# Memory attention's query projection as seven block products per head, with its weight sums made in DRAM

## The chip, the cores and the metric

The kernel runs on one core of one Trainium2 chip. The metric is the device time of one execution in microseconds, the median of several runs. The core has five engines that run their own instruction streams and meet at semaphores: TensorE (PE in the profile; its weight loads are PEld), VectorE (DVE), ScalarE (ACT), GpSimd (POOL) and SyncE (SP), which here only issues transfers. GpSimd also issues transfers, those that add to their destination among them.

## What is computed

One layer of a decoder, 512 positions wide, with 1024 channels, in float32. In short:

```python
h = rms_norm(x, norm_mix)
q_a, k_a, v_a, u_b, gate_b, gate_c, g_a, g_b = split(h @ w_in)
o_a = stick_breaking_attention(heads(q_a), heads(k_a), heads(v_a))     # 8 heads of 64, causal
y_b = gate_b * causal_conv3(gate_c * u_b)
x = x + (sigmoid(g_a) * (o_a @ w_branch_a) + sigmoid(g_b) * (y_b @ w_branch_b)) @ w_mix_out
# memory sublayer: 4 heads of 256, 256 memory tokens
q = rms_norm(x, norm_mem_q) @ w_mem_q
k, v = split(rms_norm(mem, norm_mem_kv) @ w_mem_kv)
x = x + (softmax(q @ k.T / 16) @ v) @ w_mem_o
gate, up = split(rms_norm(x, norm_ffn) @ w_ffn_in)                      # hidden width 2816
x = x + (silu(gate) * up) @ w_ffn_out
out = rms_norm(x, norm_final)
```

## The kernel before, in words

**Precision.** Every float32 operand of a matmul is split into a high part (a cast to float32r, on ScalarE) and the rest (a subtraction, on VectorE). A product is then three matmuls, high by high, high by rest and rest by high (`mm3`, lines 159 to 161). `load_w` (line 142 on) does this for a weight tile of 128 by 1024: a load on the SyncE queue into `wr` (line 146), the cast `wh` (154) and the rest `wl` (155). Each of the three tags has four buffers. `split` does it for activations (177 and 179). Activations lie transposed, channels on partitions and the 512 positions along the free dimension, so one projection of 128 output channels is 8 channel blocks x 3 terms = 24 matmuls of 512 columns (`gemm`).

**Order of the stages.** First the values of the causal attention, then the attention itself, in 16 steps (the loop at line 594). In each step TensorE works on projections (`project`) between the scores and the weighted sums, GpSimd masks (`causal`, line 415), ScalarE and VectorE make the weights. Then comes the merge loop (line 637 on), eight rounds of two gates and one branch projection, whose result is `merged`. After it, in this order: memory keys (`km`, line 662 on, eight column blocks, a 512-wide and a 256-wide part, lines 668 and 671); memory values (`vm`, two halves of four weight tiles); the mixing projection with the residual (`residual` with `w_mix_out`, line 733 on), which also makes the normalized input `x1g` of the queries; then the four heads of memory attention, the output projection with its residual (`residual` again, this time with `forms_of`), and the feed-forward.

**Memory queries.** `mem_q(h)` makes the two 128-channel blocks of head h by two plain `gemm`s (48 matmuls of 512 columns). The first head's run ahead of the loop; those of head h + 1 are emitted in head h between the softmax and the transposes of the probabilities (line 833), so that TensorE has work while VectorE finds the maxima (807) and ScalarE the exponentials (817).

**Seven products.** The feed-forward already uses, for each 2 by 2 block product, seven block products in place of eight, in a form whose partial sums are shared (Winograd's variant of Strassen's scheme). The blocks are pairs of channel blocks and halves of the positions, so a product has a free dimension of 256 (`product`, lines 913 to 921). `forms_of` (line 703 on) makes the seven activation forms, and the order of use, the PSUM banks and the evictions are written out by hand. Products 0, 3, 4 and 5 accumulate in bank `z`, 1 in `v`, 2 and 6 in `y`. Evictions copy a running sum out of `z` (line 950) between products.

**Sums in DRAM.** The seven products need sums of weight blocks. For the second feed-forward weight they are made in DRAM ahead of their use: for each of 11 column groups `sums_step` issues, in four steps, two copies on the SyncE queue (768 KB and 256 KB, line 568) and three adding transfers on the GpSimd queue (512, 256 and 256 KB, line 572), each waiting for the one before. `tick()` starts one step for up to four groups. It is called in each of the eight rounds of the merge, twice in the memory keys and four times in the first residual.

**Order on the queues.** A scheduler orders each engine's instructions by the order of emission and by estimated times, except in hand-ordered stretches such as the feed-forward; `after(i, earlier)` fixes an order without a wait.

Of the kernel before, what the change touches and what calls it, by code (L numbers as in the profile page):

```python
# [8 lines left out]
F32 = mybir.dt.float32  # L9
# [4 lines left out]
P = 128  # L14
# [28 lines left out]
def hybrid_layer(ctx: ExitStack, tc: tile.TileContext, xT_d, memT_d, mem_d, cols_d, wv_d, win_d,  # L43
# [18 lines left out]
    def nm(s):  # L62
        count[0] += 1
        return f"{s}{count[0]}"
# [490 lines left out]
        nc.gpsimd.dma_start(d.rearrange("o (t p) -> p (o t)", p=P), rm)  # L555
        return rm, d

    sums = [dpool.tile([P, 4, 512], F32, tag=f"sums{j}", name=nm("sums")) for j in range(NJ)]
    ticks = [0]

    def slots(j, i, n=1):
        return wfo_d[j].rearrange("p (s c) -> p s c", s=4)[:, i:i + n, :]

    def sums_step(j, n, *last):
        t = sums[j]
        if n == 0:
            for to, of, k in ((1, 1, 3), (0, 3, 1)):
                after(nc.sync.dma_start(t[:, to:to + k, :], slots(j, of, k)), last)
            return
        to, of = ((t[:, 0:4:3, :], slots(j, 0, 2)), (t[:, 1:2, :], t[:, 0:1, :]),  # L570
                  (t[:, 2:3, :], t[:, 1:2, :]))[n - 1]
        after(nc.gpsimd.dma_start(to, of, accum_op=ALU.add), last)  # L572

    def tick(*last):
        for n in range(3, -1, -1):
            if 0 <= ticks[0] - n < NJ:
                sums_step(ticks[0] - n, n, *last)
        ticks[0] += 1

    fill = []  # L580
    for p in range(TT):
# [9 lines left out]
    g(*args)  # L591
    scores(*steps[0])
    settle_behind()
    for i in range(len(steps) + 1):
        if i in MEM_AT:
            mem_square(MEM_AT.index(i))
        if i == MEAN_AT:
            rm, rmd = mem_factors()
        if i == ROW_AT:
            rmb = cpool.tile([P, MEM], F32, tag="rmb", name="rmb")  # L600
            after(nc.gpsimd.dma_start(rmb, rmd.broadcast_to([P, MEM])), exps[-1:])
        some = []
# [12 lines left out]
        if i > 0:  # L615
            values(*steps[i - 1])
        settle_behind(*exps[-1:], *joined[-1:])
# [44 lines left out]
    km, ready = [], []  # L662
    for m in range(KD):
        w = load_w(wmk_d[m])
        after(lows[-1], ready[m - 4:m - 3] if m > 3 else ())
        ps = mmtile("km")
        for k in range(KD):
            nc.tensor.matmul(ps, w[0][:, k, :], mgs[k], start=k == 0, stop=False,
                             skip_group_check=True)
        for k in range(KD):  # L670
            nc.tensor.matmul(ps[:, :MEM], w[1][:, k, :], mg[k][0], start=False, stop=k == KD - 1,
                             skip_group_check=True)
        t = tmp("km", MEM)
        nc.scalar.copy(t, ps[:, MEM:])
        ready.append(nc.vector.tensor_tensor(out=t, in0=ps[:, :MEM], in1=t, op=ALU.add))
        nc.vector.tensor_tensor(out=t, in0=t, in1=rmb, op=ALU.mult)
        if m % 2 == 0:
            pair = unit("kmh"), unit("kml")
        hi, lo = (u[:, (m % 2) * MEM:(m % 2 + 1) * MEM] for u in pair)
        nc.scalar.copy(hi, t)  # L680
        nc.vector.tensor_tensor(out=lo, in0=t, in1=f(hi), op=ALU.subtract)
        km.append((hi, lo))
        if m % 4 == 3:
            tick(ready[-1])
        if m == 0:
            merged.append(split(sig[0], "m"))
    vm = [[None] * 2 for _ in range(MT)]
    for n in range(2):
        pss = [ztile("vm") for _ in range(MT)]
        for c in range(4):  # L690
            w = load_w(wmv_d[n, c], 512)
            if n == 0:
                after(lows[-1], ready[c + 4:c + 5])
            for j in range(2):
                k = 2 * c + j
                for t in range(MT):
                    sl = slice(t * P, (t + 1) * P)
                    mm3(pss[t], (mg[k][0][:, sl], mg[k][1][:, sl]),
                        (w[0][:, j, :], w[1][:, j, :]), k == 0, k == KD - 1)
        for t in range(MT):  # L700
            vm[t][n] = split(pss[t], "vm", rm[:, t:t + 1])

    def forms_of(xe, xo):

# [28 lines left out]
    def residual(w_dram, act, old, gain, pairs=False):  # L733


        xs, xn = [], []
        acc = tmp("acc")
        for m in range(KD):
            w = load_w(w_dram[m])
# [6 lines left out]
                xm = old[m]  # L746
            nc.vector.tensor_tensor(out=xm, in0=ps, in1=xm, op=ALU.add)
            xs.append(xm)
            if pairs:
                raw = f(unit("xr"))  # L750
                nc.scalar.activation(raw, xm, AF.Copy, scale=gain[:, m:m + 1])
                if m % 2:
                    xn.append(forms_of(even, raw))
                else:
                    even = raw
            else:
                xn.append(split(xm, "xg", gain[:, m:m + 1]))
                if m % 2:
                    tick(lows[-1])
# [6 lines left out]
        return xs, xn, (lambda: squares_mean(acc, TT))  # L766
# [8 lines left out]
    def mem_q(h, between=None):  # L775
        got = []
        for j in range(2):
            if j and between:
                midway.append(between)
            w = load_w(wmq_d[2 * h + j])  # L780
            ps = mmtile("mq")
            gemm(ps, w, x1g)
            got.append(split(ps, "mq"))
        return got

    r1s = []
    q_next = mem_q(0, lambda: r1s.append(mean1[1]("r1", log_exp_tables(sigmoid))))
    r1 = r1s[0]
    r1s = cpool.tile([P, TT], F32, tag="r1s", name="r1s")
    nc.vector.tensor_scalar(out=r1s, in0=r1, scalar1=(D // MH) ** -0.5, scalar2=None, op0=ALU.mult)  # L790
    for h in range(MH):
        q = q_next
        scs = []
        for t2 in range(2):
            ps = ztile("sc")
# [8 lines left out]
        for t2 in range(2):  # L804
# [5 lines left out]
            nc.vector.scalar_tensor_tensor(out=nb, in0=mx, scalar=-1.0,  # L810
                                           in1=r1s[:, 2 * t2:2 * t2 + 2], op0=ALU.mult,
                                           op1=ALU.mult)
            pr = tmp("pr")
# [8 lines left out]
            for i in range(2):  # L822
                nc.vector.tensor_scalar(out=pr[:, i * MEM:(i + 1) * MEM],
                                        in0=pr[:, i * MEM:(i + 1) * MEM],
                                        scalar1=rs[:, i:i + 1], scalar2=None, op0=ALU.mult)
            prs.append(pr)
        if h + 1 < MH:
            q_next = mem_q(h + 1)
        pt = [otile("pt") for _ in range(MT)]
        for t in range(TT):  # L830
            for m in range(MT):
                c = (t % 2) * MEM + m * P
                nc.tensor.transpose(pt[m][:, t * P:(t + 1) * P], prs[t // 2][:, c:c + P], ident)
        ptr = [split(pt[m], "pt") for m in range(MT)]
        for j in range(2):
            ps = ztile("om")
            c = h * 256 + j * P
# [6 lines left out]
    x2T, x2f, mean2 = residual(wmo_d, om, x1, g_ffn, True)  # L844

# [252 lines left out]
        rest_of(*one_cast(j))  # L1098

    def w01(j):  # L1100
        return j, slots(j, 1, 2), 0, 1

    def w23(j):
        return j, sums[j][:, 0:2, :], 2, 3
# [372 lines left out]
def _layout(x, mem, norm_mix, w_in, conv_w, w_branch_a, w_branch_b, w_mix_out, norm_mem_q,  # L1477
# [12 lines left out]
    def by_pair(w):  # L1490


        return w.reshape(KD // 2, 2, P, 2, NF, P).transpose(4, 2, 3, 1, 0, 5).reshape(NF, P, 2048)

    gains = np.stack([norm_mix[0], norm_mem_q[0], norm_mem_kv[0], norm_ffn[0]])
    columns = np.concatenate([gains.reshape(4 * KD, P), conv_w[0].reshape(3 * TT, P)])
    q = w_ffn_out[0].reshape(NJ, 2, P, 2, 512)
# [11 lines left out]
        "w_mem_q": by_column(w_mem_q[0]),  # L1509
# [26 lines left out]
```

## Time and profile before

| | |
|---|---|
| median of 3 runs | 839.47 us (839.43 to 840.65) |
| the profiled execution | 839.78 us, its span 838.1 us |
| granted TensorE clock | 0.998 |
| HBM read, written | 136.74 MB, 25.17 MB |
| transfers of sums: first and last issue | 187.7 us, 370.8 us |
| query matmuls, first and last | 388.8 us, 449.0 us |

The page gives the busy time of each engine and, in forty slices, how it is spread; a matmul's own duration (about 390 ns for 512 columns) is longer than its spacing, since matmuls overlap, so spacing is read from the chain or the timeline and not from the mean duration. Busy time by stage shows which engine fills a stage. The list of waits names who waited for whom. The chain that ended last goes back from the end through whatever released each step.

### The profile page before, as it was taken

To read this page: it belongs to the slowest core of one execution; us is meant where nothing else is said; L and a number is where in the kernel's file an instruction comes from. 1 tells how busy PE (TensorE), PEld (TensorE's weight loads), DVE (VectorE), ACT (ScalarE), POOL (GpSimd) and SP (SyncE) were. 2 spreads that over 40 slices of the span, in tenths; PEclk is the share of its full clock that TensorE was granted. 3 is DMA by queue.
4 is the path that set the end of the run, shared out by engine and by line. 5 is a ranking of instruction groups with operands and counts; after the bars stand their busy time and mean duration, and the time that the engine had idled before them with its cause. 6 is when DMAs were issued, how large, how long until landed. Compare 5 with 4: busy or idle time off the path is not lost.

```text
span 838.1 us, 11942 instructions
## 1 busy us (share of the span) xinstructions
PE 829.5 (99%) x4374; PEld 713.9 (85%) x4374; DVE 662.4 (79%) x1086; ACT 463.5 (55%) x796; POOL 107.7 (13%) x131
## 2 busy tenths in 40 slices
PE   9999999999999999999999999999999999999996
PEld 7888888888888888788888889999999999888885
DVE  7879899996544466555455698999999999999886
ACT  7567868674332354444444565645555555576664
POOL 0011131111111111110000022111111110000401
PEclk9999999999999999999999999999999999999999
DMA  8552444239999999982431326667777763575552
GB/s 302 154 166 101 123 113 104 71 108 311 247 220 245 218 244 292 289 229 87 145 104 51 99 52 156 165 187 193 195 185 191 189 178 101 161 218 198 178 187 101
DMA packets 56109, 143.69 MB, mean 171 GB/s; under 512 B 6289, under 2 KB 7569, under 8 KB 56050
## 3 DMA queue, kind: packets, MB, share of 16 engines
q1 hardware_dynamic: 43410, 119.43, 43.1%
q0 software_dynamic: 12352, 23.21, 18.2%
q8 instruction: 34, 0.56, 0.3%
q10 hardware_dynamic: 288, 0.28, 0.1%
q14 instruction: 25, 0.20, 0.1%
HBM read 136.74 MB, written 25.17 MB: 193 GB/s over the span
## 4 chain that ended last, share of the span: by engine, by line
PE 95%; DMA 3%; DVE 1%; ACT 1%; issue 0%; DVEq 0%; ACTq 0%; SPq 0%
PE z L918 13%; PE p L1229 12%; PE pr L159 8%; PE pr L160 8%; PE pr L161 8%; PE y L913 5%; PE r L160 3%; PE r L159 3%; PE r L161 3%; DMA wr<-in_w_mem_v_dram 3%; PE v L286 3%; PE y L921 2%; PE v L913 2%; PE mq L161 2%; PE mq L159 2%; PE mq L160 2%
## 5 line engine op out<-in xcount | busy, mean ns | idle before, releaser
L154 ACT CAST wh<-wr 128x1024 fp32r<-128x1024 f32 x84 | 87.8, 1050 | 149.2 <-issue 71.4
L155 DVE TENSOR_TENSOR wl<-wr,wh 128x1024 fp32r<-128x1024 f32 x84 | 102.9, 1227 | 38.5 <-ACT wh L154 38.4
L159 PE MATMUL pr<-xgh,wh 128*128 128x512 f32 x288 | 112.7, 391 | 0.0
L160 PE MATMUL pr<-xgl,wh 128*128 128x512 f32 x288 | 112.4, 390 | 0.0
L161 PE MATMUL pr<-xgh,wl 128*128 128x512 f32 x288 | 112.3, 390 | 0.0
L161 PEld LDWEIGHTS pr<-xgh,wl 128*128 128x128 f32 x288 | 54.0, 188 | 11.5
L159 PEld LDWEIGHTS pr<-xgh,wh 128*128 128x128 f32 x288 | 54.1, 188 | 10.7
L160 PEld LDWEIGHTS pr<-xgl,wh 128*128 128x128 f32 x288 | 54.1, 188 | 10.5
L866 POOL DMA_DIRECT2D ws<-in_w_ffn_in_dram x22 | 26.6, 1209 | 270.4 <-DMA ws<-in_w_ffn_in_dram 55.0
L918 PE MATMUL z<-xd,wf 128*128 128x256 f32 x360 | 47.5, 282 | 0.0
L950 ACT COPY sa<-z 128x256 f32<-128x256 f32 x44 | 16.4, 374 | 51.8 <-PE z L918 51.8
L918 PEld LDWEIGHTS z<-xd,wf 128*128 128x128 f32 x360 | 45.0, 190 | 0.1
L1010 DVE TENSOR_TENSOR wf<-wg,wf 128x1024 fp32r<-128x1024 f32 (+1 forms) x44 | 43.1, 979 | 1.5
L1010 DVE TENSOR_TENSOR wl<-wr,wh 128x1024 fp32r<-128x1024 f32 x33 | 41.0, 1243 | 3.3 <-ACT wh L1077 3.3
L1077 ACT CAST wh<-wr 128x1024 fp32r<-128x1024 f32 x33 | 34.5, 1049 | 7.2 <-DMA wr<-sums 3.3
L366 DVE TENSOR_TENSOR g<-pr,r0b 128x512 f32<-128x512 f32 x16 | 11.0, 689 | 34.1 <-PE pr L161 34.1
L918 PE MATMUL z<-xf,wf 128*128 128x256 f32 x264 | 35.4, 283 | 0.0
L918 PE MATMUL z<-xc,wf 128*128 128x256 f32 x264 | 35.1, 282 | 0.0
L918 PEld LDWEIGHTS z<-xf,wf 128*128 128x128 f32 x264 | 33.4, 192 | 0.1
L918 PEld LDWEIGHTS z<-xc,wf 128*128 128x128 f32 x264 | 33.0, 190 | 0.0
L572 POOL DMA_DIRECT2D sums<-sums x22 | 19.3, 878 | 102.1 <-DMA sums<-in_w_ffn_out_dram 74.0
L1010 DVE TENSOR_TENSOR wf<-ws,wf 128x1024 fp32r<-128x1024 f32 (+1 forms) x23 | 26.9, 1171 | 0.0
(353 smaller groups left out, 2208.5 us busy)
## 6 DMA issues: line engine op xcount, KB each, us to landing
wr<-in_w_in_dram SPq DMA_DIRECT2D x36, 512.0 KB, 4.1
ws<-in_w_ffn_in_dram SPq DMA_DIRECT2D x22, 512.0 KB, 4.9
wg<-in_w_ffn_in_dram SPq DMA_DIRECT2D x22, 512.0 KB, 4.3
ws<-in_w_ffn_in_dram POOLq DMA_DIRECT2D x22, 512.0 KB, 5.9
wr<-sums SPq DMA_DIRECT2D x22, 512.0 KB, 4.2
sums<-in_w_ffn_out_dram SPq DMA_DIRECT2D x11, 768.0 KB, 10.5
wr<-in_w_ffn_out_dram SPq DMA_DIRECT2D x16, 512.0 KB, 4.5
sums<-in_w_ffn_out_dram POOLq DMA_DIRECT2D x11, 512.0 KB, 10.0
```

The costliest lines, as they stand in the source:

```text
L154: after(nc.scalar.copy(h2, raw), lead[-1:])
L155: lows.append(nc.vector.tensor_tensor(out=l2, in0=raw, in1=f(h2), op=ALU.subtract))
L159: nc.tensor.matmul(ps, a[0], b[0], start=start, stop=False, **kw)
L160: nc.tensor.matmul(ps, a[0], b[1], start=False, stop=False, **kw)
L161: nc.tensor.matmul(ps, a[1], b[0], start=False, stop=stop, **kw)
L286: nc.tensor.matmul(vps[t], xg[k][a][:, sl], wv[k][b], start=k == 0 and (a, b) == (0, 0), stop=k == KD - 1 and a == 1)
L866: nc.gpsimd.dma_start(s13, a[:, 0:4:3, :], accum_op=ALU.add)
L913: nc.tensor.matmul(ps, hi, both[0], start=i < 3 and k == 0, stop=False, skip_group_check=True)
L918: nc.tensor.matmul(ps[:, :HS], a, b, start=i < 3 and k == 0 and j == 0, stop=k == KP - 1 and j == 2, skip_group_check=True)
L1010: nc.vector.tensor_tensor(out=lo, in0=src, in1=f(hi), op=ALU.subtract)
L1077: nc.scalar.copy(hi, raw)
L1229: nc.tensor.matmul(res[i][s2], a[:, ts], b, start=j == 0 and n == 0, stop=n == 2 and j == (BEHIND - 1 if (i, s2) == (5, 1) else NJ - 1))
```

## The change

The diff does five things.

1. **Queries as seven products.** For each head the 1024 by 256 weight is taken as 2 by 2 blocks (rows in pairs of channel blocks, columns in two halves of 128), and the product with the activations, also in 2 by 2 blocks (pairs of channel blocks, halves of the positions), is made as 7 products x 4 row pairs x 3 terms, all of 256 columns. `q_product` issues one product and its eviction. Its order in a head is 0, 1, 3, 2, 4 (`mem_q_first`) and, later, 5, 6 (`mem_q_last`). The first matmul of a product is ordered behind the product before it (`turn`), as are the transposes between `mem_q_first` and `mem_q_last` of the next head. The sign of every second key block is turned, to match a form that comes out negated.
2. **Forms of the activations.** `flat_forms` makes the seven forms in the first residual, as `forms_of` does in the second.
3. **Forms of the weights.** Each head's weight sums are made in DRAM by two copies and three adding transfers (`form_sums`), started in the attention loop: head h's copies at step 2 + 2h, and each adding step two steps of the loop later. `pair_forms` loads and splits three and a half tiles of 128 by 1024 a head, in place of two.
4. **When the output sums run.** `tick` is now called at every step of the attention loop, in every round of the merge, once per head and four times in the second residual; it is no longer called in the keys and in the first residual. Of the 11 groups of the second feed-forward weight, the first five start in the merge, one a round from the first on; the other six start at its last round, the four heads, and the second residual's first call.
5. **Order of the stages.** The mixing projection with its residual now comes right behind the merge, whose last `merged` tile is split in the merge itself. Then come the keys, the first half of the values, the first five products of head 0, half of the second half of the values, products 5 and 6, and the rest of the values. The keys take their banks from the pool of four and no longer from the pool of two.

The core of it, lines left out at "...":

```diff
+    def form_sums(t, src):
+        w = quarters(src)
+        return ([copied(t[:, 0:2, :], w[:, 0:2, :]), copied(t[:, 2:4, :], w[:, 1:3, :])],
+                [added(t[:, 0:2, :], w[:, 3:4, :].broadcast_to([P, 2, 512]))],
+                [added(t[:, 2:3, :], t[:, 0:1, :])], [added(t[:, 3:4, :], t[:, 2:3, :])])
...
+    qsums = [in_dram(f"qsums{h}") for h in range(MH)]
+    for h in range(MH):
+        job(2 + 2 * h, form_sums(qsums[h], wmq_d[h]), 2)
+    for j in range(5):
+        job(len(steps) + 1 + j, out_sums(j))
+    for j in range(5, NJ):
+        job(len(steps) + 3 + j, out_sums(j))
+
     for i in range(len(steps) + 1):
+        tick(*exps[-1:])
...
-        if m < KD - 1:
-            merged.append(split(sig[0], "m"))
+        merged.append(split(sig[0], "m"))
         tick(sigmoid)
...
-        if m % 4 == 3:
-            tick(ready[-1])
-        if m == 0:
-            merged.append(split(sig[0], "m"))
...
-    x1, x1g, mean1 = residual(wmix_d, merged, None, g_q)
+    x1, x1f, mean1 = residual(wmix_d, merged, None, g_q, flat_forms)
...
+    def q_product(h, i):
+
+        if i == 0:
+            qbanks[h] = {"z": ztile("qz"), "t": tmp("qa"), "u": tmp("qb"), "s": tmp("qs")}
+        elif i in (1, 2):
+            qbanks[h]["vy"[i - 1]] = mmtile("qv")
+        b = qbanks[h]
+        ps = b["zvyzzzy"[i]][:, :HS]
+        for k in range(KD // 2):
+            hi, lo = (w[:, k * P:(k + 1) * P] for w in forms_w[h, i])
+            xh, xl = x1f[k][i]
+            for j, (u, x) in enumerate(((hi, xh), (hi, xl), (lo, xh))):
+                mm = nc.tensor.matmul(ps, u, x, start=i < 3 and k + j == 0,
+                                      stop=k == KD // 2 - 1 and j == 2, skip_group_check=True)
+                if k + j == 0:
+                    after(mm, turn[-1:])
+        turn.append(mm)
...
+        if i == 0:
+            qacts.append(nc.scalar.copy(s[:, :HS], ps))
+        elif i == 1:
+            nc.vector.tensor_tensor(out=t[:, :HS], in0=ps, in1=s[:, :HS], op=ALU.add)
+        elif i == 3:
+            qacts.append(nc.scalar.copy(s[:, HS:], ps))
+        elif i == 4:
+            qacts.append(nc.scalar.copy(u[:, HS:], ps))
...
+        elif i == 6:
+            nc.vector.tensor_tensor(out=t[:, HS:], in0=ps, in1=s[:, HS:], op=ALU.add)
+            qgot[h][0] = split(t, "mq")
...
-        ps = mmtile("km")
+        ps = ztile("km")
...
+    values_part(0, (0, 1, 2, 3))
+    for n in range(3):
+        pair_forms(0, n)
+    mem_q_first(0)
+    values_part(1, (0, 1))
+    q_product(0, 5)
+    q_product(0, 6)
+    values_part(1, (2, 3))
+    for n in range(2):
+        pair_forms(1, n)
...
+        if 0 < h + 1 < MH:
+            pair_forms(h + 1, 2, bound)
+        tick(*casts[-1:])
         if h + 1 < MH:
-            q_next = mem_q(h + 1)
+            mem_q_first(h + 1)
...
+        if h + 1 < MH:
+            mem_q_last(h + 1)
```

More of the change, by code (lines that the diff above doesn't have):

```diff
@@ L556, in mem_factors, with quarters, in_dram, copied @@
         return rm, d
[L558 to L572, printed above, removed]
+    def quarters(w):
+        return w.rearrange("p (s c) -> p s c", s=4)
+    def in_dram(tag):
+        return dpool.tile([P, 4, 512], F32, tag=tag, name=nm(tag))
+    sums = [in_dram(f"sums{j}") for j in range(NJ)]
+    def copied(to, of):
+        return lambda *last: after(nc.sync.dma_start(to, of), last)
+    def added(to, of):
+        return lambda *last: after(nc.gpsimd.dma_start(to, of, accum_op=ALU.add), last)
+    def out_sums(j):
+        t, w = sums[j], quarters(wfo_d[j])
+        return ([copied(t[:, 1:4, :], w[:, 1:4, :]), copied(t[:, 0:1, :], w[:, 3:4, :])],
+                [added(t[:, 0:4:3, :], w[:, 0:2, :])], [added(t[:, 1:2, :], t[:, 0:1, :])],
+                [added(t[:, 2:3, :], t[:, 1:2, :])])
+    def form_sums(t, src):
[3 more added lines that the diff above has]
+                [added(t[:, 2:3, :], t[:, 0:1, :])], [added(t[:, 3:4, :], t[:, 2:3, :])])
+    jobs, started = {}, [0]
+    def job(at, steps, lag=1):
+        for n, some in enumerate(steps):
+            jobs.setdefault(at + n * lag, []).extend(some)
     def tick(*last):
[L575 to L578, printed above, removed]
+        for some in jobs.pop(started[0], ()):
+            some(*last)
+        started[0] += 1
     fill = []
@@ L748, in residual @@
             xs.append(xm)
[L749 to L755, printed above, removed]
-            else:
-                xn.append(split(xm, "xg", gain[:, m:m + 1]))
-                if m % 2:
-                    tick(lows[-1])
+            if old is not None and m % 2:
+                tick(lows[-1])
+            raw = f(unit("xr"))
+            nc.scalar.activation(raw, xm, AF.Copy, scale=gain[:, m:m + 1])
+            if m % 2:
+                xf.append(formed(even, raw))
+            else:
+                even = raw
             if m == 0:
@@ L765, in residual @@
                 nc.vector.tensor_tensor(out=acc, in0=acc, in1=sq, op=ALU.add)
[L766 to L768 removed]
+        return xs, xf, (lambda: squares_mean(acc, TT))
+    x1, x1f, mean1 = residual(wmix_d, merged, None, g_q, flat_forms)
     mean1 = mean1()
     fpool = ctx.enter_context(tc.tile_pool(name="fpool", bufs=2))
[L773 to L784 removed]
@@ L786, in hybrid_layer, with pair_forms @@
-    r1s = []
-    q_next = mem_q(0, lambda: r1s.append(mean1[1]("r1", log_exp_tables(sigmoid))))
+    forms_w = {}
+    def pair_forms(h, n, *last):
+        t, w = qsums[h], quarters(wmq_d[h])
+        src, which = ((w[:, 1:3, :], (0, 1)), (t[:, 2:4, :], (3, 6)), (t[:, 0:2, :], (2, 4)),
+                      (w[:, 0:1, :], (5,)))[n]
+        raw = wpool.tile([P, 2, 512], F32, tag="wr", name=nm("wr"))
+        if n == 3:
+            both = wpool.tile([P, 2, 512], F32R, tag=("wh", "wl")[h % 2], name=nm("wf"))
+            raw, hi, lo = raw[:, 0:1, :], both[:, 0:1, :], both[:, 1:2, :]
+        else:
+            hi, lo = (wpool.tile([P, 2, 512], F32R, tag=t, name=nm("wf")) for t in ("wh", "wl"))
+        nc.sync.dma_start(raw, src)
+        after(nc.scalar.copy(hi, raw), qacts[-1:])
+        after(nc.vector.tensor_tensor(out=lo, in0=raw, in1=f(hi), op=ALU.subtract), last)
+        for n, i in enumerate(which):
+            forms_w[h, i] = hi[:, n, :], lo[:, n, :]
@@ new lines, in mem_q_first, with mem_q_last @@
+    def mem_q_first(h):
+        q_product(h, 0)
+        pair_forms(h, 3)
+        q_product(h, 1)
+        q_product(h, 3)
+        q_product(h, 2)
+        q_product(h, 4)
+    def mem_q_last(h):
+        q_product(h, 5)
+        if h + 1 < MH:
+            pair_forms(h + 1, 0)
+        q_product(h, 6)
+        if h + 1 < MH:
+            pair_forms(h + 1, 1)
+    qacts, turn, km, ready = [], [], [], []
+    r1s = []
+    for m in range(KD):
+        w = load_w(wmk_d[m])
+        after(lows[-1], ready[m - 4:m - 3] if m > 3 else ())
+        ps = ztile("km")
+        for k in range(KD):
+            nc.tensor.matmul(ps, w[0][:, k, :], mgs[k], start=k == 0, stop=False,
+                             skip_group_check=True)
+        for k in range(KD):
+            nc.tensor.matmul(ps[:, :MEM], w[1][:, k, :], mg[k][0], start=False, stop=k == KD - 1,
+                             skip_group_check=True)
+        t = tmp("km", MEM)
+        nc.scalar.copy(t, ps[:, MEM:])
+        ready.append(nc.vector.tensor_tensor(out=t, in0=ps[:, :MEM], in1=t, op=ALU.add))
+        nc.vector.scalar_tensor_tensor(out=t, in0=t, scalar=1.0 - 2 * (m % 2), in1=rmb,
+                                       op0=ALU.mult, op1=ALU.mult)
+        if m % 2 == 0:
+            pair = unit("kmh"), unit("kml")
+        hi, lo = (u[:, (m % 2) * MEM:(m % 2 + 1) * MEM] for u in pair)
+        nc.scalar.copy(hi, t)
+        nc.vector.tensor_tensor(out=lo, in0=t, in1=f(hi), op=ALU.subtract)
+        km.append((hi, lo))
+        if m == 1:
+            r1s.append(mean1[1]("r1", log_exp_tables(sigmoid)))
```

109 lines of the change are left out of this document (66 added, 43 removed).

## The prediction

> **What bounds the kernel now.** I read the page's engine totals and slices first, then busy time by stage, then the waits of TensorE, then the chain that ended last.
>
> ```profile
> span 838.1 us, 11942 instructions
> PE 829.5 (99%) x4374; PEld 713.9 (85%) x4374; DVE 662.4 (79%) x1086; ACT 463.5 (55%) x796; POOL 107.7 (13%) x131
> ```
>
> ```profile
> 40.00:160.00 120.00, 120.00 (x572) 101.43 (x571) 107.35 (x185) 87.83 (x170) 22.03 (x43) 1.00 0.43 117
> 185.00:300.00 115.00, 115.00 (x509) 95.20 (x508) 60.28 (x78) 41.40 (x57) 20.07 (x21) 1.00 0.97 247
> 300.00:367.00 67.00, 66.27 (x321) 55.51 (x320) 41.98 (x59) 31.96 (x47) 11.39 (x12) 1.00 1.02 280
> 411.00:463.00 52.00, 51.95 (x277) 43.87 (x275) 27.82 (x55) 22.41 (x48) 1.25 (x1) 1.00 0.34 102
> 463.00:504.00 41.00, 41.00 (x183) 33.74 (x183) 31.72 (x58) 23.64 (x45) 8.60 (x6) 1.00 0.31 77
> ```
>
> The columns of the second fence are the stretch, its length, then PE, PE's weight loads, VectorE, ScalarE and GpSimd busy, the granted clock, the DMA share and GB/s. TensorE is busy in all of attention (40 to 160), in the merge (185 to 300) and in the last projection (463 to 504). It is idle for 0.73 us in memory keys and values (300 to 367), where the DMA engines are full (1.02), and for 0.05 us among the heads. The clock is whole everywhere. So the kernel is bound by the sum of its matmuls; only fewer matmul microseconds, or new waits, can move its time.
>
> ```profile
> PE vm L160 <- DVE wl L155: 0.6, 1, 0.6
> ```
>
> ```profile
> 300.05 1.81 PE km L668 x8
> 301.86 0.95 PE km L671 x8
> 302.81 1.84 PE km L668 x8
> 314.06 12.58 DMA wr<-in_w_mem_v_dram
> 330.09 10.12 DMA wr<-in_w_mem_v_dram
> ```
>
> ```profile
> 510.96 4.31 PE z L918 x36
> ```
>
> The one wait of TensorE after the start is in the values stage. The chain there runs back through two value weights that took 12.58 and 10.12 us to arrive. The chain also gives the pace: a 512-wide matmul costs 1.81/8 to 1.84/8, so 0.226 to 0.230 us; a 256-wide one 0.95/8 = 0.119, and in the feed-forward products, which have the form that the change introduces, 4.31/36 = 0.1197 us.
>
> **The change, part by part.**
>
> ```profile
> L159 PE MATMUL mq<-xgh,wh x64: 387/389/476, 388.8 to 448.5; 128*128 128x512 f32 x64
> L161 PE MATMUL mq<-xgh,wl x64: 389/389/397, 389.3 to 449.0; 128*128 128x512 f32 x64
> ```
>
> *Query matmuls.* Lines 159, 160 and 161 hold 64 each (the first and last of three equal rows are shown): 192 x 0.228 = 43.8 us. The change makes 4 heads x 7 products x 4 row pairs x 3 terms = 336 matmuls of 256 columns: 336 x 0.1197 = 40.2 us. Gain 3.6 us, by the ends of the pace 3.2 (0.226) to 4.0 (0.230). All of it lies on TensorE and so on the path.
>
> The Trainium skill ("TensorE: Matmul & The Clock Gate", Back-to-back issue gap) speaks against the change. It gives a sustained pace, with weight loads, of about 131 ns for 512 columns and 81 ns for 128, from which I estimate 98 ns for 256; 336 x 98 is 7.8 us more than 192 x 131. The chain above disagrees: 0.228 and 0.120 us, nearly in proportion, and the measurement decides.
>
> *The stall at the values.* All sum transfers leave this stage: the ticks in the keys' loop go, and those of the first residual move to the second. Then the weights alone use the DMA engines. The 0.73 us of idle time should go, nearly whole; I take 0.7 (bounds 0 and 0.8). What is late next is the weights' cast, bounded below.
>
> ```profile
> L154 ACT CAST wh<-wr 128x1024 fp32r<-128x1024 f32 x84 | 87.8, 1050 | 149.2 <-issue 71.4
> L155 DVE TENSOR_TENSOR wl<-wr,wh 128x1024 fp32r<-128x1024 f32 x84 | 102.9, 1227 | 38.5 <-ACT wh L154 38.4
> L950 ACT COPY sa<-z 128x256 f32<-128x256 f32 x44 | 16.4, 374 | 51.8 <-PE z L918 51.8
> ```
>
> ```profile
> L681 DVE TENSOR_TENSOR kml<-km,kmh 128x256 fp32r<-128x256 f32 x8 | 3.4, 425 | 9.0 <-ACT kmh L680 9.0
> L747 DVE TENSOR_TENSOR x<-r,x 128x512 f32<-128x512 f32 x3 | 2.1, 686 | 1.2 <-PE r L161 1.2
> ```
>
> *Weight casts per head.* Before: two weight tiles, 2 x 1.05 on ScalarE and 2 x 1.23 on VectorE. After: three and a half, so 1.6 and 1.8 us more per head. Seven products also bring four 256-wide copies on ScalarE (4 x 0.37 = 1.5 us) and three 256-wide sums on VectorE (3 x 0.42, by the next fence). In 411 to 463 VectorE is busy 27.8 of 52 and ScalarE 22.4, so both have room; nothing on the path, as long as no TensorE instruction waits in line behind a cast.
>
> *Mixing projection straight into the keys.* The new forms add work to VectorE at the join: the last pair costs five 256-wide operations of 0.42 and three 512-wide ones of 0.69, the last sum, square and the split for the mean four more of 0.69: 7.0 us. The keys need 8 x (1.23 + 3 x 0.42) = 19.9 us of VectorE beside 8 x (1.83 + 0.95) = 22.2 us of TensorE. Three weights can be cast ahead (four buffers), the first value weight must be added: 7.0 + 19.9 - 3.7 + 1.2 = 24.4 against 22.2. By these durations TensorE loses up to 2.2 us.
>
> ```profile
> 110.41 0.61 DVE L511 SCALAR_TENSOR_TENSOR al<-a,r,ah 128x384 fp32r<-128x384 f32 x1
> 110.94 0.69 DVE L430 TENSOR_TENSOR l<-e,l 128x512 fp32r<-128x512 f32 x1
> 111.55 0.69 DVE L179 TENSOR_TENSOR yl<-gb,yh 128x512 fp32r<-128x512 f32 x1
> ```
>
> But back to back VectorE starts an operation before the last one's record ends: 0.61 for 0.69, 0.53 for 0.61, a factor of 0.88. Then 24.4 is 21.5, under 22.2. I take 0.3 (0 to 2.2). At the join before it, the last merged tile must be multiplied, added and split (four steps of about 0.69, 2.8 us) while the projection's first seven operands run, 21 x 0.228 = 4.8 us: nothing, as long as that cover stands; without it 2.8.
>
> ```profile
> SPq L146 <- DVE wl L155: 74.5, 26, 5.4
> SPq L224 <- ACT vrow L215: 1.3, 1, 1.3
> SPq L226 <- DMA row<-vrow: 1.2, 1, 1.2
> ```
>
> With the projection its eight weights, its eight tiles of x and the mean's row move ahead of the keys on the SyncE queue, and the mean's two matmuls into the keys. The row's store and load hold the queue for 1.3 + 1.2 us; key weights stand behind them now, one needed each 2.8 us, but the queue mostly waits for a free buffer (74.5 us from 300 to 400), which means that it runs a buffer round ahead: nothing, or 2.5 without that lead.
>
> *Reuse of one bank.* Products 0, 3, 4 and 5 accumulate in one bank, so product 3 waits for ScalarE's copy of product 0 and has only product 1 (12 x 0.12 = 1.4 us) as cover. Queued ahead of that copy are the softmax's exponentials:
>
> ```profile
> 405.03 0.40 PE L161 MATMUL mq<-xgh,wl 128*128 128x512 f32 x1
> ```
>
> ```profile
> 407.47 0.20 ACT L817 ACTIVATION_READ_ACCUMULATOR pr<-sc,nb,r1s 128x1 f32 x1
> ```
>
> In the first head they end 2.6 us after the scores (407.67 against 405.03); the copy then ends at 3.0, and product 3 would start at 2 x 1.43 = 2.9. So 0.1 us in three heads: 0.3; if a 1.05 us cast slips in ahead of the copy, 1.1 each, 3.3 (bounds 0 and 3.3). The scores of the next head wait for product 6's sum, cast and rest, 0.42 + 2 x 0.69 = 1.8 us, under 12 matmuls of the output, 2.7 us: nothing, and 0.3 each if a cast (1.23) is queued in between.
>
> *The sums.*
>
> ```profile
> q1 hardware_dynamic: 43410, 119.43, 43.1%
> q0 software_dynamic: 12352, 23.21, 18.2%
> sums<-in_w_ffn_out_dram SPq DMA_DIRECT2D x11, 768.0 KB, 10.5
> ```
>
> ```profile
> L572 POOL DMA_DIRECT2D sums<-sums x22: 805/830/1335, 206.6 to 370.8; - x22
> L572 POOL DMA_DIRECT2D sums<-in_w_ffn_out_dram x11: 1172/1172/1482, 197.3 to 356.2; - x11
> ```
>
> One set is 1 MB copied and 1 MB added. Plain transfers moved 119.4 MB in 0.431 x 838 us of all 16 engines, 3.0 us a MB; adding ones 23.2 MB in 0.182 x 838, 6.6 us a MB. A set costs 9.6 us of DMA. Four sets go into attention (the stretch 40 to 160, where 38 us more raise the share from 0.43 to 0.75); six of the eleven output sets go from the full stage into heads and last projection (about 93 us at 0.33, plus 58, so about 0.95). The full stage of before shows the price of that: 0.73 us of TensorE in 67. I take 0.2 (0 to 0.8) for the waits that remain. On the SyncE queue the copies stand ahead of weight loads that are fetched several products early.
>
> On GpSimd each query set adds 1.17 + 2 x 0.83 = 2.8 us, 11.3 in all, among the causal masks. GpSimd is busy 22.0 of 120 us there, so I take nothing (0 to 11.3, below). At the feed-forward's start its own adds come behind the sums' last ones:
>
> ```profile
> 488.65 1.21 POOL L866 DMA_DIRECT2D ws<-in_w_ffn_in_dram  x1 [13.55 <-DVE xo L724]
> 500.65 1.73 POOL L878 TENSOR_TENSOR wg<-ws,wg 128x512 f32<-128x512 f32 x1 [7.56 <-DVE wf L1010]
> ```
>
> The second add is issued 12 us before its consumer; one held-up sum is covered.
>
> *Sum.* -3.6 - 0.7 + 0.3 + 0.3 + 0.2 = -3.5 us. The profiled execution took 839.78 around its span of 838.1, 0.3 over the median of 839.47; so 836.3 for such an execution and 836.0 for the median.
>
> **Rivals.** *New waits eat the gain.* The cast in front of the copy in two heads (2.2 in place of 0.3), the scores (0.9), half of the join (1.1 in place of 0.3) and the sums (0.2) make +4.4 against -4.3: no change, 839.6. For it: each product has a shorter cover than the 24-matmul chain it replaces. Against: the feed-forward runs the same seven products and the list of waits shows none there.
>
> *Slower: GpSimd in attention.*
>
> ```profile
> 112.22 0.39 PE L504 MATMUL z<-l,negtri 128*128 128x512 f32 x1
> ```
>
> An add that stands in front of a mask, or waits there for its copy to land, delays VectorE behind the mask; VectorE is busy 107 of 120 us. The rest shown above ends at 111.63 and TensorE uses it at 112.22: 0.6 us of slack. To be slower overall the twelve adds must cost 3.5 + 1.7 = 5.2 us, 0.43 each past the slack, so hold a mask for about 1.0 us. At their full length, 11.3, the time is 836.0 + 11.3 = 847. Against it: two of the loop's 16 steps lie between a copy and its first add (attention fills about 150 us, so some 19 us), and a copy lands in 10.5 even under full load; GpSimd is free for four fifths of the stage.
>
> The Trainium skill ("SBUF — State Buffer", SBUF: two separate sides) says that a GpSimd-issued transfer is held up while VectorE uses the shared port, 620 ns becoming 3100. It would make this rival likely. The page's row of the feed-forward's adds, under a busier VectorE, tells against it:
>
> ```profile
> L866 POOL DMA_DIRECT2D ws<-in_w_ffn_in_dram x22 | 26.6, 1209 | 270.4 <-DMA ws<-in_w_ffn_in_dram 55.0
> ```
>
> 1.21 us there, 1.17 in the half-idle stage.
>
> *The narrow matmuls do not pay.* If a 256-wide matmul cost over 43.8/336 = 0.130 us, the products would lose; at 0.14 they take 47.0 us in place of 40.2, and the sum gives 836.0 + 6.8 = 842.8. The rows say 0.120, so hardly any chance; this is the case of the matmul page too.
>
> **How the numbers follow.** A measurement of this kernel can tell about 0.2%, 1.7 us, from no change. Forecast (835 to 837.8): 0.62. More gained, as several small waits among the heads go too (833 to 835): 0.08. Gain eaten (837.8 to 841.2): 0.18. GpSimd: 0.10. Narrow matmuls: 0.02. So faster 0.70, same 0.18, slower 0.12. The range runs from 834.0, which leaves out half of the second case, to 840.0, which leaves out the slower ones and a third of the eaten gain.
>
> **What would show it.** Right: 336 query matmuls at 0.12 us; keys and values with no DMA in the chain; TensorE idle under 1 us outside the start; sums at 0.95 DMA share late in the heads. Wrong: TensorE waiting on ScalarE's copies in the query products, on VectorE's weight rests in the keys, or in attention on rests behind a GpSimd mask; or a pace above 0.13 us.

## The result, and the profile after

The change makes the kernel slower: 852.32 us median (850.92 to 853.6) against 840.04 (839.43 to 840.65) beside it, a ratio of 1.0146 [1.0123, 1.0169]. The profiled execution of after took 853.42 us. The views answer to those of before, in the same order: engine totals, stages (length, then PE, PE's weight loads, VectorE, ScalarE, GpSimd busy, granted clock, DMA share, GB/s), and TensorE's waits.

```profile
span 851.6 us, 12376 instructions
PE 831.6 (98%) x4518; PEld 721.8 (85%) x4518; DVE 682.1 (80%) x1130; ACT 483.3 (57%) x836; POOL 117.5 (14%) x143
```

```profile
40.00:160.00 120.00, 118.67 (x564) 99.89 (x564) 106.56 (x182) 87.48 (x170) 30.93 (x55) 1.00 0.78 186
185.00:300.00 115.00, 115.00 (x511) 95.33 (x510) 61.76 (x81) 43.69 (x59) 15.59 (x17) 1.00 0.83 219
300.00:367.00 67.00, 67.00 (x323) 56.51 (x322) 50.92 (x91) 39.60 (x65) 2.03 (x2) 1.00 0.46 131
411.00:463.00 52.00, 51.53 (x363) 47.32 (x362) 37.02 (x70) 31.25 (x66) 7.28 (x7) 1.00 0.86 256
463.00:504.00 41.00, 39.87 (x179) 32.70 (x177) 21.09 (x39) 16.89 (x32) 9.62 (x10) 1.00 0.91 173
...
499.00:525.00 26.00, 15.99 (x68) 13.26 (x68) 19.68 (x35) 13.83 (x29) 9.08 (x7) 0.74 0.50 87
...
510.00:515.00 5.00, 3.18 (x10) 2.65 (x10) 4.82 (x8) 2.33 (x4) 1.88 (x2) 0.50 0.02 5
```

```profile
PE z L1046 <- ACT xf L699: 4.6, 2, 3.2
PE z L1046 <- DVE xf L700: 3.6, 2, 2.7
PE v L1041 <- DVE x L752: 1.8, 1, 1.8
...
PE z L458 <- issue: 1.3, 1, 1.3
PE qz L808 <- ACT qs L815: 0.5, 1, 0.5
```

The middle of the kernel is as full as before, and the stage at 300 to 367 fuller (67.00 of 67). Apart from a wait of 1.3 us in attention, TensorE is idle in one place that was full before, 499 to 525: 15.99 us busy of 26. The first three rows of the waits, 4.6 + 3.6 + 1.8 = 10.0 us, are those of the first feed-forward products for their activation forms. While it waits, the clock falls to 0.50.

Where the time went, by the first matmul of a stage in the two traces:

| first matmul of | before | after | the stretch up to it |
|---|---|---|---|
| the merge's branch (`br`) | 191.1 | 193.5 | +2.4 |
| the feed-forward (`z`) | 503.72 | 502.00 | -4.1 |
| the feed-forward's output (`p`) | 722.5 | 736.0 | +15.2 |
| end of the span | 838.1 | 851.6 | 0.0 |

So the middle gained 4.1 us, about what was forecast, the stretch before it lost 2.4, and the start of the feed-forward lost 15.2. TensorE there (start, us, line, instruction, then the wait):

```profile
502.00 0.87 PE L1046 MATMUL z<-xf,wf 128*128 128x256 f32 x6
506.11 0.45 PE L1046 MATMUL z<-xf,wf 128*128 128x256 f32 x1 [3.24 <-ACT xf L699]
509.27 0.80 PE L1046 MATMUL z<-xf,wf 128*128 128x256 f32 x2 [2.71 <-DVE xf L700]
511.88 1.65 PE L1041 MATMUL v<-xo,wf 128*128 128x512 f32 x3 [1.82 <-DVE x L752]
```

What made the forms late stands on ScalarE and GpSimd:

```profile
503.99 0.62 ACT L1027 CAST wf<-ws 128x512 fp32r<-128x512 f32 x1 [15.55 <-DMA ws<-in_w_ffn_in_dram]
```

```profile
467.96 0.85 POOL L570 DMA_DIRECT2D sums<-sums  x1 [10.16 <-DMA sums<-sums]
471.43 0.81 POOL L570 DMA_DIRECT2D sums<-sums  x1 [2.61 <-DMA sums<-in_w_ffn_out_dram]
471.97 1.47 POOL L570 DMA_DIRECT2D sums<-in_w_ffn_out_dram  x1
484.00 0.88 POOL L570 DMA_DIRECT2D sums<-sums  x1 [10.56 <-DMA sums<-sums]
488.01 0.82 POOL L570 DMA_DIRECT2D sums<-sums  x1 [3.13 <-DMA sums<-in_w_ffn_out_dram]
493.13 1.66 POOL L570 DMA_DIRECT2D sums<-sums  x2 [4.29 <-DMA sums<-sums]
494.18 1.88 POOL L994 DMA_DIRECT2D ws<-in_w_ffn_in_dram  x1
```

```profile
473.89 1.21 POOL L866 DMA_DIRECT2D ws<-in_w_ffn_in_dram  x1 [52.87 <-DVE c L711]
488.65 1.21 POOL L866 DMA_DIRECT2D ws<-in_w_ffn_in_dram  x1 [13.55 <-DVE xo L724]
```

The last fence is GpSimd before the change. The feed-forward's add for its first column block went out at 473.89 then; now it goes out at 494.18, 20.3 us later, since the adds of the sums, seven of them in the fence above, stand ahead of it on GpSimd's queue and wait, one behind the other, for transfers to land. (The load that it adds to landed at 473.3 us before and at 477.3 now, so 16.9 of the 20.3 us are the queue's.) Its own landing takes 9.74 us more (the chain has it: `494.18 9.74 DMA ws<-in_w_ffn_in_dram`). ScalarE casts that tile in order, so it sits idle for 15.55 us, and behind it stand `xr` (line 757, at 504.52) and the forms of the residual's later blocks, which the first products need.

### The profile page after: what moved, and what is told of

Its sections match the earlier page's. It is cut to its first block, busy times and chain, and to the rows that moved or that the text cites. A ratio compares the mean times of both kernels' runs of the same rounds, so it can differ in the third digit from the quotient of the medians.

```text
span 851.6 us, 12376 instructions
## 1 busy us (share of the span) xinstructions
PE 831.6 (98%) x4518; PEld 721.8 (85%) x4518; DVE 682.1 (80%) x1130; ACT 483.3 (57%) x836; POOL 117.5 (14%) x143
## 4 chain that ended last, share of the span: by engine, by line
PE 88%; DMA 7%; DVE 3%; issue 1%; ACT 1%; POOL 0%; SPq 0%; DVEq 0%; POOLq 0%; ACTq 0%
PE z L1046 12%; PE p L1357 12%; PE pr L159 8%; PE pr L160 8%; PE pr L161 8%; PE y L1041 5%; DMA sums<-sums 2%; PE y L1049 2%; PE v L1041 2%; PE v L286 2%; PE qz L808 2%; DMA ws<-in_w_ffn_in_dram 2%; DMA sums<-in_w_ffn_out_dram 2%; PE km L856 2%; PE r L161 2%; PE r L159 2%
## 5 line engine op out<-in xcount | busy, mean ns | idle before, releaser
L154 ACT CAST wh<-wr 128x1024 fp32r<-128x1024 f32 x76 | 79.9, 1053 | 110.6 <-issue 45.1
L155 DVE TENSOR_TENSOR wl<-wr,wh 128x1024 fp32r<-128x1024 f32 x76 | 93.3, 1227 | 11.3 <-ACT wh L154 11.3
L159 PEld LDWEIGHTS pr<-xgh,wh 128*128 128x128 f32 x288 | 54.1, 188 | 10.6
L1046 PE MATMUL z<-xf,wf 128*128 128x256 f32 x264 | 37.7, 290 | 8.2 <-ACT xf L699 4.6
L1138 DVE TENSOR_TENSOR wl<-wr,wh 128x1024 fp32r<-128x1024 f32 x33 | 41.1, 1246 | 3.8 <-ACT wh L1205 3.7
L1205 ACT CAST wh<-wr 128x1024 fp32r<-128x1024 f32 x33 | 34.6, 1052 | 6.6 <-DMA wr<-sums 3.1
L570 POOL DMA_DIRECT2D sums<-in_w_ffn_out_dram x11 | 14.7, 1333 | 157.2 <-DMA sums<-in_w_ffn_out_dram 157.2
```

The source lines that it names most:

```text
L154: after(nc.scalar.copy(h2, raw), lead[-1:])
L155: lows.append(nc.vector.tensor_tensor(out=l2, in0=raw, in1=f(h2), op=ALU.subtract))
L159: nc.tensor.matmul(ps, a[0], b[0], start=start, stop=False, **kw)
L570: return lambda *last: after(nc.gpsimd.dma_start(to, of, accum_op=ALU.add), last)
L1046: nc.tensor.matmul(ps[:, :HS], a, b, start=i < 3 and k == 0 and j == 0, stop=k == KP - 1 and j == 2, skip_group_check=True)
L1138: nc.vector.tensor_tensor(out=lo, in0=src, in1=f(hi), op=ALU.subtract)
```

## The experiments

Two theories: the loss is a queue, adds of the sums that wait for landings ahead of the feed-forward's adds (Q in the later expectations); or it is bandwidth, the DMA engines simply have too much to move late, at a share of 0.86 and 0.91 in the last two stages (B there). The runs are told in the order of the argument.

**All output sums early.** From the merge on, one group a step; the four steps of the second residual go back to the first.

```diff
-    for j in range(5):
+    for j in range(NJ):
         job(len(steps) + 1 + j, out_sums(j))
-    for j in range(5, NJ):
-        job(len(steps) + 3 + j, out_sums(j))
...
-            if old is not None and m % 2:
+            if old is None and m % 2:
                 tick(lows[-1])
```

> The change, but all eleven output sums start one a tick from the merge's first round on; the ticks of the second residual go back to the first residual, so the last step of the last group runs in the heads (tick 30) and the second residual has no sum on any queue. Theory Q (the feed-forward's own adding transfers stand in GpSimd's queue behind sums that wait for their landings) and theory B (the DMA engines are simply full there) both expect the 15 us at the feed-forward's start to go: 836 to 838, with TensorE idle under 0.5 us between 499 and 525, and a full DMA stage again in merge and first residual that may cost up to 0.7 us. A theory that the loss lies in the query products expects 850.

837.37 us (836.19 to 842.69, twelve runs), ratio 0.9981 [0.9967, 0.9995]. TensorE's waits:

```profile
PE qz L806 <- ACT qs L813: 0.5, 1, 0.5
PE z L458 <- issue: 0.2, 1, 0.2
```

```profile
471.08 1.21 POOL L992 DMA_DIRECT2D ws<-in_w_ffn_in_dram  x1 [22.92 <-DVE c L692]
485.13 1.20 POOL L992 DMA_DIRECT2D ws<-in_w_ffn_in_dram  x1 [12.84 <-DVE xo L704]
```

With the late adds gone, the feed-forward's adds go out at 471.08 and 485.13 and the whole stall goes. As many bytes are moved as in after, so it is their place that costs. This does not yet tell the queue from bandwidth late in the kernel.

**Only the queue's order.** The sums stay where the change has them, but the feed-forward's first add is put ahead of the adds of the last three steps.

```diff
+        if m == 0:
+            for late in late_adds:
+                after(late, [i])
```

> The change with one thing moved: on GpSimd's queue the adding transfer of the feed-forward's first column block stands ahead of the sums' adds of ticks 30 to 32, and no longer behind them. All transfers remain, in the same stage. Theory Q (it is the place in the queue: in the changed kernel that add's destination was loaded at 477.3 us and the add was issued at 494.2) expects the add at about 478, the wait at the feed-forward's start to shrink from 10 us to under 4, and 838 to 845. Theory B (the DMA engines are full, so the add would land late anyway) expects 848 to 853.

841.28 us (838.88 to 847.82, ten runs), ratio 1.0032 [1.0013, 1.005].

```profile
473.13 1.22 POOL L1001 DMA_DIRECT2D ws<-in_w_ffn_in_dram  x1 [0.98 <-DVE xc L713]
...
498.35 1.52 POOL L1001 DMA_DIRECT2D ws<-in_w_ffn_in_dram  x1
```

```profile
PE z L1056 <- DVE xf L707: 1.9, 1, 1.9
...
PE z L1056 <- ACT xf L706: 0.6, 1, 0.6
```

The same transfers in another order bring the median from 852.32 to 841.28 us and the ratio from 1.0146 to 1.0032. The add goes out at 473.13, and the DMA share from 463 to 504 stays at 0.92 (0.91 in after). What is left, 2.5 us of waits and a half clock behind them, leads back to the next add and to GpSimd's own sum `wg` behind it, which still stand behind the sums (498.35 and 499.11; before 488.65 and 490.10). So the queue, and not the bytes, makes most of this loss: that is shown.

**Late adds as copies.** From step 28 of the sums on (the last head and the second residual), each add is replaced by two plain copies on the SyncE queue.

```diff
+            for _ in range(2):
+                spare = dpool.tile([P, 2, 512], F32, tag=nm("spare"), name=nm("spare"))
+                after(nc.sync.dma_start(spare[:, :of.shape[1], :], of), last)
```

> The change, but each adding step that starts from tick 28 on (the last head and the second residual, 12 of them) is replaced by two plain copies of its source to spare DRAM on SyncE, about the same DMA time (two copies at 3.0 us a MB for one add at 6.6). These sums are left out, so the output projection of the feed-forward uses unfinished sums for six groups; its time is not touched by the values. GpSimd's queue is then free in the second residual while the DMA engines stay as loaded. Theory Q expects the start of the feed-forward to be whole again, 837 to 839. Theory B expects the stall to stay, 848 to 853.

853.44 us, ratio 1.0176 [1.0155, 1.0197]. It was to tell Q from B and did not. Its time lies in the range that B expected, but the waits show another queue:

```profile
PE r L159 <- ACT wh L154: 6.2, 1, 6.2
PE z L1052 <- DVE xf L706: 1.9, 1, 1.9
```

The copies wait for the sums that they read, and on the SyncE queue the weights of the last projection stand behind them: the same stall, moved to another queue.

**The late sums in the feed-forward.** The second residual's four steps go behind the activations of column blocks 2, 4, 6 and 8.

```diff
-            if old is not None and m % 2:
-                tick(lows[-1])
...
+            if m in (2, 4, 6, 8):
+                tick(silus[-1])
```

> The change, but the four ticks of the second residual are put into the feed-forward, behind the silu of its column blocks 2, 4, 6 and 8. The heads keep their four ticks. Both theories on the feed-forward's start expect it to go: 836 to 838; it also shows what the same waits cost inside the feed-forward, where GpSimd's own adds come every 9.7 us: up to 2 us if a sum's wait holds one of them.

843.66 us (839.91 to 846.46), ratio 1.0055 [1.0039, 1.007]. The start is whole, but there is a new wait, in the profiled run (839.91 us, the fastest of the six) at 583 us:

```profile
PE z L1039 <- ACT sb L1076: 3.4, 1, 3.4
```

There the feed-forward's own adds landed after 17.7 and 11.2 us. In both places tried beside adds that others wait for, the sums are paid for.

**The sums in attention alone.** Before, with four sets of copies and adds like those of the queries in attention, of which nothing is used.

```diff
+    for h in range(MH):
+        t = dpool.tile([P, 4, 512], F32, tag=f"qsums{h}", name=nm("qsums"))
+        for n, some in enumerate(form_sums(t, wfo_d[h])):
+            jobs.setdefault(2 + 2 * h + 2 * n, []).extend(some)
```

> The kernel before, with four sets of sums like those of the queries made in the attention loop at the same steps and lags as in the change, from other weights, and not used. It prices the moved sums in attention alone. If the wait of 1.3 us in front of the scores at 146.7 us in the changed kernel comes from transfers (head tiles moved between partitions that land late behind the copies), the kernel gets slower by 1.0 to 2.0 us, with a wait of TensorE before scores. If it was chance, no difference. If GpSimd's masks were the cause, waits show on VectorE's rests in front of TensorE instead.

846.47 us (841.03 to 847.23), ratio 1.0076 [1.0056, 1.0096].

```profile
149.06 0.63 PE L458 MATMUL z<-qk,qk 128*128 128x128 f32 x4 [3.39 <-issue]
...
151.35 0.63 PE L159 MATMUL pr<-xgh,wh 128*128 128x512 f32 x1
151.78 0.63 PE L160 MATMUL pr<-xgl,wh 128*128 128x512 f32 x1
```

The scores wait 3.39 us, and the matmuls behind them come every 0.43 us in place of 0.227. In after the same matmul waits 1.33 us, at 146.73. The tiles it reads come by moves on the SyncE queue; in after, then in before:

```profile
L359 SPq DMA_DIRECT2D qk<-qk x5: 461/462/587, 129.8 to 144.4; - x5
...
DMA to landing us min/median/max: 4.5/7.7/8.0
```

```profile
L359 SPq DMA_DIRECT2D qk<-qk x2: 461/462/462, 128.1 to 134.2; - x2
...
DMA to landing us min/median/max: 2.2/4.8/7.3
```

The last moves go out 10 us later and land more slowly; the masks are not what TensorE waits for. So the sums have a price in attention too, here more than the 1.0 to 2.0 us that were expected. It differs between executions: four other versions with the same sums in attention (the first four told above) send the last move at 141.2 to 142.5 us, and TensorE waits 0.2 us there in one of them and not at all in three.

**Without query sums.** The early version, whose seven products read plain weight blocks.

```diff
-        t, w = qsums[h], quarters(wmq_d[h])
+        t = w = quarters(wmq_d[h])
```

> The early output sums, without any query sums: the products read plain weight blocks in their place (the sums of the query weights are left out, the number and size of loads and matmuls is unchanged). It prices what the query sums cost in the first experiment. If attention's cost is theirs, 835.0 to 836.5 with a narrow spread; if the spread has another cause, 837 as before.

836.33 us (835.95 to 836.89, five runs), ratio 0.9963 [0.9951, 0.9976]: a gain of 3.1 us, with 0.9 us between the runs. That is what the products, with the stage order, are worth with their query sums for nothing. The early version's spread (6.5 us) is wider, but it comes from two of twelve runs (841.35 and 842.69); that the query sums make it is not shown by five runs without them.

**The stage order alone.** Before, with memory keys and values behind the mixing projection, the same matmuls as before.

> The kernel before with only the order of the stages changed: the last merged tile split in the merge, the mixing projection ahead of keys and values; plain queries, output sums as before. It prices the order alone. If the seven products bring the gain of the first experiment (3.6 us of matmuls), this one stays within 1 us of the kernel before. If the order brings it (the idle 0.7 us in the values and waits around the projections), it gains 1 us or more.

839.19 us, ratio 0.9993 [0.9985, 1.0002]: no difference that the runs can tell. The edit moves the stages and nothing else, so no diff is shown. Most of the gain is then the seven products'. In this run's trace keys and values take 44.1 us (44.2 in after), where they took 45.4 before, so some of it can be the order's.

**Query sums elsewhere.** Four versions of the early one, which differ in the steps at which the query sums of heads 0 to 3 start (attention has the steps 0 to 16, the merge 17 to 24):

```diff
-        job(2 + 2 * h, form_sums(qsums[h], wmq_d[h]), 2)
+        job((1, 2, 11, 13)[h], form_sums(qsums[h], wmq_d[h]), 2)                  # first
+        job((2, 4, 17, 18)[h], form_sums(qsums[h], wmq_d[h]), (2, 2, 1, 1)[h])    # second
+        job(len(steps) + 1 + h, form_sums(qsums[h], wmq_d[h]))                    # third
+        job((2, 4, 11, 13)[h], form_sums(qsums[h], wmq_d[h]), 2)                  # fourth
```

In the second and third the output sums start two steps later.

> The early output sums (first experiment), and the query sums moved away from the steps in which the last pair's query and key tiles are moved between partitions: heads 0 and 1 start at steps 1 and 2, heads 2 and 3 at steps 11 and 13 (two steps between parts as before). If the spread of 836 to 843 of the first experiment comes from those moves landing late behind copies, the spread goes and the median is 835.5 to 836.5. If the query sums cost through GpSimd's masks or by DMA load as such, it stays at 837 with its spread.

First: 838.29 us (838.01 to 840.75), ratio 0.9991 [0.9982, 1.0]. That is over the 835.5 to 836.5 that were expected. There is no wait for the moves; there is a new one at 86 us, for a rest that VectorE makes, and why it is late stays open:

```profile
PE o L523 <- DVE al L511: 0.8, 2, 0.5
```

> The version with all output sums from the merge on, and the query sums of heads 2 and 3 moved out of attention: they start at the first two ticks of the merge, and the eleven output sums two ticks later, so that the last add is asked for in the last head. Theory Q (the loss was the queue of adds at the feed-forward's start; what is left of the price lies in attention, where moves of query and key tiles are held up behind the copies of heads 2 and 3): the wait in attention at 120 to 150 us goes, the last adds are asked for before 450 us and land some 25 us ahead of the feed-forward's first add, so 836.3 to 836.9 and a spread under 1.5 us. Rival B (bandwidth: what counts is how much the DMA engines move in all, wherever it lies): the merge, whose DMA share is 0.98 already, now waits for its weights, 0.5 to 2 us of idle TensorE between 185 and 345, so 837.5 to 839.

Second: 838.07 us (836.43 to 840.42), ratio 0.9976 [0.9962, 0.9989]. Attention waits no more than 0.2 us, but the spread is 4 us and the values wait for a weight's rest. The time is in the range that B expected (837.5 to 839) and not in that of Q, while the wait lies behind the stretch that B named (185 to 345), so this run settles neither. TensorE's waits, then its matmuls behind them:

```profile
PE vm L160 <- DVE wl L155: 1.3, 1, 1.3
...
PE vm L159 <- DVE km L861: 0.4, 1, 0.4
```

```profile
370.34 0.63 PE L160 MATMUL vm<-wl,mg 128*128 128x512 f32 x1
370.77 0.63 PE L161 MATMUL vm<-wh,mg 128*128 128x512 f32 x1
```

> As the run beside it, but all four query sums start in the merge, one a tick, the first two output sums sharing a tick with the last two of them. Attention then holds no sums, as before the change. Theory Q: as the version without query sums in attention, 836.1 to 836.7 and a spread of about 1 us. Rival B: the merge takes two sets (19 us of DMA) more than in the run beside it at a share of 0.98, so it is 1 us or more slower than that one, and TensorE waits for branch or residual weights between 185 and 345.

Third: 849.44 us (846.22 to 851.77), ratio 1.0109 [1.0086, 1.0132]. This is what B expected: the DMA share is 1.02 from 185 to 300, loads of the mixing projection, issued in the merge, land after 19 us, and that projection waits:

```profile
wr<-in_w_mix_out_dram SPq DMA_DIRECT2D x7, 512.0 KB, 19.0
```

```profile
PE r L159 <- ACT mh L177: 3.1, 1, 3.1
```

> The version with all output sums from the merge on; the query sums of heads 0 and 1 start at attention's steps 2 and 4 as in the change, those of heads 2 and 3 at steps 11 and 13, behind the moves of the last query and key tiles (121 to 137 us in the run that moved all four). Theory Q: neither the masks at 86 us (where steps 1 and 2 cost 0.8 us) nor the moves are held up, so TensorE waits nowhere in attention, 836.3 to 837.2, spread under 1.5 us. Rival B (bytes moved): the merge, at a DMA share of 0.98, takes the last adds of heads 2 and 3 in addition, and its weights or those of the first residual come late as when all query sums lay there: over 838, with idle TensorE between 185 and 370.

Fourth: 836.99 us (836.29 to 838.5), ratio 0.9967 [0.9955, 0.998].

```profile
PE qz L806 <- ACT qs L813: 0.5, 1, 0.5
```

```profile
40.00:160.00 120.00, 120.00 (x572) 101.34 (x571) 107.80 (x184) 87.98 (x171) 27.23 (x50) 1.00 0.71 170
185.00:300.00 115.00, 115.00 (x509) 95.27 (x508) 60.27 (x78) 41.98 (x57) 21.79 (x24) 1.00 1.03 261
```

The one wait left after the start is that of the query products. Nothing waits in attention or in the merge, although the merge's DMA share is 1.03, as high as in the third version; but the loads of the mixing projection land after a median of 9.4 us here, in place of 19.0. The spread is 2.2 us, where under 1.5 was expected. This version beats before, and after by 15 us, with the change's transfers all in it. Against the early version (0.9981 [0.9967, 0.9995]) the intervals overlap.

## Why the prediction was wrong

**The matmuls** (-3.6). The pace was right: twelve from 419.94, the next at 421.38, 0.120 us each.

```profile
419.94 1.60 PE L808 MATMUL qz<-xf,wf 128*128 128x256 f32 x12
421.38 0.28 PE L808 MATMUL qv<-xfh,wf 128*128 128x256 f32 x1
```

Summed from start to start, the query matmuls took 43.9 us before and 41.5 after, a gain of 2.5: 336 x 0.1197 = 40.2, plus 1.3 of gaps, one of them the wait of 0.5 on ScalarE's copy, which the **bank reuse** (0.3) had foreseen. The Trainium skill ("TensorE: Matmul & The Clock Gate", Back-to-back issue gap), from which I had estimated 98 ns and a loss, is contradicted by these rows.

**The stages before the heads** (-0.7 for the stall, +0.3 for the join). From start to start the values took 22.7 us before and 21.8 after, the keys 22.7 and 22.3, the two residuals 87.8 and 87.5. The stall went, the join cost nothing and the keys even gained 0.4. Casts, scores and the merged tile cost nothing either, as forecast. The forecast of matmuls and stages without the sums, -3.7, met a measured -4.1, in part by luck: the products with their bank gave 2.5 us where 3.3 was forecast, and the other stages 1.6 where 0.4 was. With the stage order alone the stall goes too (90.00 us of TensorE in the 90 from 300 to 390), so that part is not the products'.

**The sums** (0.2, bounds 0 and 0.8) are the step that failed. I priced them by the DMA share and by what a full stage had cost TensorE before; the shares came out near the forecast (0.95 against 0.86 and 0.91), the price did not. The sentence that failed is "The second add is issued 12 us before its consumer; one held-up sum is covered." The add that decided is the one ahead of it, at 473.89, which I looked past. Its tile was cast at 492.81 before the change, a cover of 18.9 us with its landing in it. And not one sum but the dependent adds of several stood ahead, each waiting for a landing (10.16 and 10.56 us before two of them); with the load under it, which landed 3.9 us later, that made it 20.3 us late. The waits of 10.0 us and the halved clock behind them make 15.2. The reordered run shows it: with every transfer kept, the stretch from the first `z` to the first `p` takes 223.5 us (500.32 to 723.8), where it took 218.8 before and 234.0 in after: a loss of 4.7 us in place of 15.2.

**GpSimd in attention** (0, and the slower rival at 847). The rival named the right queue and the wrong place: no wait for a mask is in after's list, though the first add of a query set held GpSimd for a median of 1.36 us and once for 2.39, where 1.17 was taken. In attention TensorE lost 1.3 us to the moves of query and key tiles in after's profile, and 0 to 0.2 in the four others with the same sums there. Of the 2.4 us before the merge, 0.8 is there before the first query sum is issued (the first weighted sum starts at 56.84 before and at 57.60 after; in the other versions at 57.0 to 57.9), so about 1.6 is attention's. That the moves are late because of the copies is read from the traces (the last one goes out at 133.5 to 135.0 us in the four versions without sums in attention, and at 141.2 to 146.5 in the six with them at the change's steps); which of the queue's order and the fuller DMA engines delays them stays open.

The rival of new waits in the products themselves (839.6) fell: they cost 0.5 us.

## What to carry to other kernels

A transfer that waits for another's landing holds everything behind it on its engine's queue, so a chain of such transfers is priced by its waits and by who stands behind it, not by its bytes; look for the next consumer of that queue, and for all of its instructions, before you move such a chain. A DMA share near 1 does not say how late transfers land: two versions here had 1.02 and 1.03 in the merge, with loads that landed after 19.0 and 9.4 us, and only the first waited for them. And microseconds are lost at a lower share (0.78 in attention) where small moves are needed within a few. When you count a gap in TensorE, look at the granted clock behind it.

## What the runs showed of the hardware

A gap of TensorE can cost more than its length. With the waits of 3.24, 2.71 and 1.82 us the granted clock was 0.50 from 506.3 to 516.5 us, and once more from 519.9 to 523.3, and the 15.2 us lost hold only 10.0 of waits. The Trainium skill ("TensorE: Matmul & The Clock Gate", Part 1: The HAM clock gate) has the clock halve after an idle window of about 3.4 us; the 3.39 us wait in the version with the sums in attention alone comes near that and was followed by half a clock. But the wait of 3.42 us at 583 us, with the late sums in the feed-forward, left the clock whole (the column before the last two):

```profile
580.00:590.00 10.00, 6.70 (x43) 5.90 (x44) 9.25 (x17) 5.28 (x9) 1.24 (x1) 1.00 0.92 194
```

And in the second version above waits of 1.33 and 0.41 us within 2.5 us were followed by matmuls 0.43 us apart, while the single wait of 1.33 us in after's attention left the spacing at 0.227. So the length of a wait alone does not decide it; what does, no run here shows.

The adding transfers of 512 KB, which landed in 10.0 us before, took a median of 17.6 us to land from 440 to 500 in after, and 10.6 in the version with the feed-forward's add put first, at the same DMA share of 0.95 there. Why they differ stays open. In after:

```profile
sums<-in_w_ffn_out_dram POOLq DMA_DIRECT2D x3, 512.0 KB, 17.6
```
